# A hybrid decoder layer on one core: instructions kept in the order issued, the third weight sum in another tile, dependent work one piece later, one normalisation chain

## The chip, the cores and the metric

The kernel runs on one core of one Trainium2 chip. The metric is the device time of one execution in microseconds, given as the median of several runs. In the texts below PE is the matrix engine, DVE the vector engine, ACT the scalar engine, POOL the GpSimd engine and SP the engine from which most DMAs are issued. The engines run side by side, each through its own queue of instructions in order, and wait for one another by semaphores.

## The reference

The reference is one layer over 272 positions (16 learned ones and 256 given ones) of 4096 channels: a norm, one projection to 16384 columns, two branches (stick-breaking attention and a gated short convolution, sixteen heads of 128 each), each multiplied by a gate and normalised per head, and one projection back, added to the input and normalised.

```python
h = rmsnorm(x, norm_g)
p = h @ w_in                                   # 272 x 4096 by 4096 x 16384
q, k, v, g_attn, b_conv, c_conv, h_conv, z_conv = jnp.split(p, cuts, axis=-1)
o = stick_breaking_attention(heads(q), heads(k), heads(v))
o = group_rmsnorm(o * jax.nn.silu(g_attn), attn_norm_g, ATTN_HEADS)
y = b_conv * short_conv(c_conv * h_conv, conv_w)
y = group_rmsnorm(y * jax.nn.silu(z_conv), conv_norm_g, CONV_GROUPS)
hs = x + jnp.concatenate([o, y], axis=-1) @ w_out
return rmsnorm(hs, final_norm_g)[:, N_META:]
```

All in fp32. Attention takes, for each query, weights worked out from the scores by a logarithm, a reversed running sum and an exponential.

## The kernel before

**Pieces.** The weights come as a list of pieces, 128 x 1024 numbers each, and one loop (L916) goes through the list. Piece `i` is multiplied in round `i`; its load was issued eight pieces ahead (`LOADS`), its split five ahead (`SPLITS`). A split (`split`, L345) makes two fp32r tiles out of an fp32 piece: `wh`, a cast by ACT (L381), and `wl`, what the cast left out, a subtraction by DVE (L382). Each product is then three matmuls: `wh` with both parts of the activations, `wl` with the large one (L414, L416, L417 for rows, L406 to L408 for blocks). The raw tiles have five buffers, `wh` and `wl` six.

**Kinds of pieces.** The columns q, gate, b and z of a pair of heads (a *group*, eight in all) are computed with positions as rows. Two row blocks of the weight make a *pair*. A plain pair is two pieces A and B of four products each, twelve matmuls a piece. A "seven" pair uses a scheme with seven products in place of eight: A (2), B (1), T (2), U (2). T and U are not loaded but summed by DVE from A's and B's raw tiles, in three sums (L391, L394, L395): T into a tile `t` that has one buffer, U back into A's raw tile. The columns k, v, c and h of each head are computed with channels as rows: a *block* of 272 or 258 positions, in four *quarters* p of 8 row blocks, 24 matmuls each. Pieces x give the norm's statistics, pieces m load the mixed output of a group back, and eight pieces o make the last thin output columns.

**Zones.** A group from the second on begins with zone R: four plain pairs, between them the last four half blocks of the group before (its second head's c and h), sixteen pieces, called f+1 to f+16 after the last piece f of the group before. Then comes zone S, twelve *slots*, numbered 0 to 11, each the A, B, T and U of a seven pair and two quarters of a block, so that a block ends in every odd slot: k, v, c, h of the first head and k, v of the second. After the last group stand its last two blocks (zone Z), and then the second projection, with its own pairs.

**Work around the pieces.** At the end of a block `plain_block` reads its PSUM bank by DVE: `kT` (L545), `vt` (L551), `cc` (L567), and `cc` multiplied (L572) for the block h. After the last plain piece `open_rows` copies one finished bank into `cb` (ACT, L604); at the end of the group `evict` reads the others. The rest is done in tasks. `later(at, fn)` puts one down for round `at`, and `run_tasks`, the last call of each round, issues those that are due, each whole. `plan_group` (L777) sets the rounds. For group g: `silu` and the transposes `qT` at f+1; for each of its two heads `scores`, `weights`, `trans` and `po`, the second head's at f+10, f+13, f+15 and f+18; the normalisation of its attention part (`norm`, "h") at f+20. In zone S of the group after: `conv_t` (four transposes `ct`) in slot 2, `conv_out` (POOL) one round on, the normalisation of its convolution part ("c") and the mix of h (`mxh`) in slot 4, the mix of c (`mxc`) in slot 8. The last group has rounds of its own.

`trans` transposes the attention weights in blocks of 32 (DVE) and moves the blocks to their places in `at` by sixteen ACT copies (L538); `po` (L740 to L744) multiplies them with `vv`, the transposed v, which comes by sixteen copies of the same kind and four of `v3` (L560) after each v block. A `norm` is four squares (ACT, L653), a chain of eleven small DVE operations (L655, `rsqrt_raw`, L657) and four multiplications (ACT, L660). A `mix` is four transposes on PE (L666), whose result ACT multiplies by the norm's weights (L677) and sends to memory.

**PSUM banks.** In zone S seven banks hold the group's products, and the eighth, the *spare* bank, is taken in turn by each block and by the transposes `ct`, `mxh`, `mxc` and the second head's `po`. A new user waits until the one before has been read.

**What sets the order.** The instructions of an engine do not run in the order in which the code issues them: the framework's scheduler puts each engine's queue in an order of its own, by its estimate of when each instruction's operands are ready. A waiting instruction holds all behind it in that queue.

Of the kernel before, what the change touches and what calls it, by code (L numbers as in the profile page):

```python
# [110 lines left out]
def kernel(ctx, tc, xt, xin, xm, par, fg, w1, w2, out):  # L111
# [124 lines left out]
    def small(nm):  # L236
        return [wk.tile([P, 4], F32, tag=f"sm{i}", name=f"{nm}{i}") for i in range(3)]
# [9 lines left out]
    xr, kept = {}, {}  # L247
# [30 lines left out]
    def late_sums(j):  # L278
# [5 lines left out]
        token_sums(d, t, j)  # L284
        kept[j] = d

    def lend(j):

        nc.sync.dma_start(out=sumd[j], in_=kept.pop(j).bitcast(F32))

    def token_sums(dst, t, j):
# [7 lines left out]
        v.tensor_tensor(out=f[:, 3, :], in0=a12, in1=f[:, 1, :], op=ALU.add)  # L299
        nc.scalar.copy(out=dst[:, 0], in_=f)  # L300
# [44 lines left out]
    def split(i):  # L345
# [9 lines left out]
        if p[0] == "m":  # L355
# [4 lines left out]
            for q in range(2):  # L360
                j = 2 * p[1] + q
                if j in OUT_SJ:
# [4 lines left out]
                    token_sums(S2[j], t[:, 2 * q:2 * q + 2], f"o{j}")  # L367
# [8 lines left out]
        else:  # L376
            h = wp.tile([P, 1024], F32R, tag="wh", name=f"wh{i}", bufs=RING)
            lo = wp.tile([P, 1024], F32R, tag="wl", name=f"wl{i}", bufs=RING)
        for q in range(parts):
            c = slice(q * w // parts, (q + 1) * w // parts)  # L380
            nc.scalar.copy(out=h[:, c], in_=t[:, c])  # L381
            nc.vector.tensor_tensor(out=lo[:, c], in0=t[:, c], in1=h[:, c].bitcast(F32), op=ALU.subtract)  # L382
        splits[i] = (h, lo)
        if two and p[0] == "A":
            sums[p] = t
        elif two:
# [7 lines left out]
            nc.vector.tensor_tensor(out=a[:, c2], in0=a[:, c2], in1=s[:, c1], op=ALU.add)  # L394
            nc.vector.tensor_tensor(out=a[:, c1], in0=t[:, c1], in1=a[:, c2], op=ALU.add)  # L395
            sums[("T",) + p[1:]], sums[("U",) + p[1:]] = s, a

# [92 lines left out]
    tasks = []  # L490
# [4 lines left out]
    def run_tasks(i):  # L495
        ready = [t for t in tasks if t[0] <= i]
        for t in ready:
            tasks.remove(t)
        for t in sorted(ready, key=lambda t: t[0]):
            t[1](*t[2])  # L500
# [3 lines left out]
    def finish_stats():  # L504
        sst = wk.tile([P, 4], F32, tag="sm3", name="sst")
# [42 lines left out]
    def v_block(u, src, at_):  # L548
# [4 lines left out]
        def vtrans():  # L553
            y = wk.tile([P, 416], F32, tag="zs", name=f"yv{u}")
            V.transpose(out=y[:, :L + META], in_=vt[:, :L + META])
            vv = wk.tile([P, 2 * P], F32, tag=f"vv{u % 2}", name=f"vv{u}")
# [88 lines left out]
    def norm(g, q):  # L645

        y = gr[g][q][1]
        f = 0 if q == "h" else 4
        ss = wk.tile([P, 4], F32, tag="sm3", name=f"ss{q}{g}")
        j = wk.tile([P, P], F32, tag="junk", name=f"j{q}{g}")  # L650
        for t in range(2):
            for u in range(2):
                A.activation(out=j, in_=y[:, t, u], func=AF.Square, scale=(rt if q == "h" else rt2)[:, t:t + 1],  # L653
                             accum_out=ss[:, 2 * u + t:2 * u + t + 1])
        V.tensor_scalar(out=ss, in0=ss, scalar1=1.0 / P, scalar2=None, op0=ALU.mult)  # L655
        r = rsqrt_raw(ss, 4, EPS, *small(f"n{q}{g}_"))
        V.tensor_tensor(out=ss, in0=r, in1=fac[:, f:f + 4], op=ALU.mult)  # L657
        for t in range(2):
            for u in range(2):
                A.mul(out=y[:, t, u], in_=y[:, t, u], mul=ss[:, 2 * u + t:2 * u + t + 1])  # L660
# [23 lines left out]
    def q_t(g):  # L684
        q = gr[g]["h"][0]
        o = bank(f"qT{g}")
        for u in range(2):
            for t in range(2):
                c = (2 * u + t) * P
                T.transpose(out=o[:, c:c + P], in_=q[:, t, u], identity=ident)  # L690
        A.copy(out=q, in_=o.rearrange("p (u t x) -> p t u x", u=2, t=2))

    def scores(g, u):
# [4 lines left out]
        T.matmul(out=z[:, 144:ZW], lhsT=q[:, 1, u], rhs=kt, start=True, stop=True)  # L698
        zm = wk.tile([P, 448], F32, tag="zm", name=f"zm{g}_{u}")[:, :ZW]
# [18 lines left out]

# [10 lines left out]
    def trans(g, u):  # L729
        za = gr[g].pop(("za", u))  # L730
        y = wk.tile([P, 448], F32, tag="zl", name=f"ya{g}_{u}")
        V.transpose(out=y, in_=za)
        blocks(at[:, P:], y[:, :3 * P], 3)
# [16 lines left out]
    def conv_t(us):  # L750
        o = bank(f"ct{us[0]}")
        for n, u in enumerate(us):
            for t in range(2):
                T.transpose(out=o[:, n * SEQ + t * P:n * SEQ + (t + 1) * P], in_=cy[u][:, t * P:(t + 1) * P], identity=ident)
# [292 lines left out]
```

## Time and profile before

| | |
|---|---|
| median of 3 runs | 1840.49 us (1839.96 to 1843.44) |
| profiled execution, its own time | 1845.58 us |
| its span, first to last instruction | 1843.9 us |
| mean granted clock of PE | 0.994 |
| DMA | 393.64 MB, 213 GB/s on average |

The profile describes one execution, which took 5.1 us longer than the median of the runs. Its page gives the busy time of each engine as a share of the span. The groups list the instructions of one line, engine and operation, with the busy time and the mean duration of one, and then the idle time just before them and which engine's work ended it. A timeline row has the start in us, the duration, engine, line, operation and tiles (`out<-in`), and how many instructions it holds. A windows row has for each engine its busy time in that stretch (PE, weight loads, DVE, ACT, POOL), the granted clock of PE as a share of full speed, the DMA engines' share and GB/s.

### The profile page before, as it was taken

What the parts mean: (1) busy time and instruction counts of PE and PEld (TensorE: products, weight loads), DVE (VectorE), ACT (ScalarE), POOL (GpSimd) and SP (SyncE); (2) the same over time, 40 slices, a digit from 0 to 9 for tenths busy, and PEclk for the clock granted to TensorE, in tenths of its full rate; (3) what the DMA queues carried; (4) which work ended last, traced back from release to release, by engine and by line L of the source; (5) the groups of instructions that cost most, each with busy time, mean ns of one, the idle gap of its engine ahead of it and who ended that gap; (6) DMA issues with size and microseconds to landing.
All of it is one profiled execution on the core that took longest, in us unless ns stands there. A gap on an engine that the chain in (4) does not pass through costs nothing.

```text
span 1843.9 us, 29709 instructions
## 1 busy us (share of the span) xinstructions
PE 1793.4 (97%) x10998; PEld 1618.1 (88%) x10998; DVE 1493.0 (81%) x1946; ACT 1201.2 (65%) x2012; POOL 154.2 (8%) x192
## 2 busy tenths in 40 slices
PE   9999999999999999999999999999999998999997
PEld 7899888988898889888988898889888976888897
DVE  6765788778877887888788877887788878998986
ACT  6755875686568656865776577657765785554554
POOL 2150010101010101010101010101010231000000
PEclk9999999999999999999999999999999999999999
DMA  8867467746765677467746674667466774675655
GB/s 308 318 237 239 162 195 235 230 169 198 225 225 175 199 230 231 165 206 226 239 161 209 222 235 166 210 211 234 161 211 212 236 271 160 228 227 191 208 180 194
DMA packets 116065, 393.64 MB, mean 213 GB/s; under 512 B 13008, under 2 KB 18256, under 8 KB 115920
## 3 DMA queue, kind: packets, MB, share of 16 engines
q1 hardware_dynamic: 111888, 388.08, 64.2%
q10 hardware_dynamic: 4032, 3.67, 0.6%
q8 instruction: 86, 1.41, 0.3%
q14 instruction: 59, 0.48, 0.1%
HBM read 380.17 MB, written 11.53 MB: 212 GB/s over the span
## 4 chain that ended last, share of the span: by engine, by line
PE 74%; DVE 9%; issue 5%; ACT 5%; DMA 3%; POOL 2%; SPq 0%; ACTq 0%; DVEq 0%; POOLq 0%
PE P L414 14%; PE P L416 14%; PE P L417 14%; PE mm L406 10%; PE mm L407 10%; PE mm L408 10%; DVE wl L382 4%; ACT wh L381 3%; DMA raw<-w 2%; DVE t L391 1%; DVE raw L395 1%; DVE raw L394 1%; ACT at L538 1%; POOL cb L643 1%; PE mo L860 0%
## 5 line engine op out<-in xcount | busy, mean ns | idle before, releaser
L382 DVE TENSOR_TENSOR wl<-raw,wh 128x1024 fp32r<-128x1024 f32 (+3 forms) x756 | 846.0, 1150 | 228.3 <-ACT wh L381 219.0
L381 ACT CAST wh<-raw 128x1024 fp32r<-128x1024 f32 (+3 forms) x756 | 708.1, 974 | 385.8 <-DVE raw L395 213.2
L406 PE MATMUL mm<-xs,wh 128*128 128x258 f32 (+1 forms) x2048 | 584.9, 286 | 0.0
L408 PE MATMUL mm<-xs,wl 128*128 128x258 f32 (+1 forms) x2048 | 581.7, 284 | 0.6 <-DVE wl L382 0.6
L407 PE MATMUL mm<-xs,wh 128*128 128x258 f32 (+1 forms) x2048 | 581.9, 284 | 0.0
L406 PEld LDWEIGHTS mm<-xs,wh 128*128 128x128 f32 x2048 | 385.6, 188 | 5.8 <-issue 0.6
L407 PEld LDWEIGHTS mm<-xs,wh 128*128 128x128 f32 x2048 | 385.7, 188 | 4.4
L408 PEld LDWEIGHTS mm<-xs,wl 128*128 128x128 f32 x2048 | 385.6, 188 | 0.8 <-DVE wl L382 0.8
L414 PE MATMUL P<-wh,xs 128*128 128x512 f32 x604 | 237.6, 393 | 1.5 <-ACT wh L381 1.5
L417 PE MATMUL P<-wl,xs 128*128 128x512 f32 x604 | 235.7, 391 | 0.7 <-DVE wl L382 0.5
L416 PE MATMUL P<-wh,xs 128*128 128x512 f32 x604 | 235.7, 390 | 0.0
L391 DVE TENSOR_TENSOR t<-raw,raw 128x1024 f32<-128x1024 f32 (+1 forms) x108 | 130.2, 1206 | 32.5 <-DMA raw<-w 32.3
L381 ACT CAST wh<-t 128x1024 fp32r<-128x1024 f32 (+1 forms) x108 | 112.0, 1037 | 58.9 <-DVE t L391 21.7
L414 PE MATMUL P<-wh,mixl 128*128 128x512 f32 (+1 forms) x392 | 148.4, 379 | 0.0
L416 PE MATMUL P<-wh,mixh 128*128 128x512 f32 (+1 forms) x392 | 147.5, 377 | 0.0
L417 PE MATMUL P<-wl,mixh 128*128 128x512 f32 (+1 forms) x392 | 147.2, 377 | 0.0
L382 DVE TENSOR_TENSOR wl<-t,wh 128x1024 fp32r<-128x1024 f32 (+1 forms) x108 | 130.8, 1211 | 6.9 <-ACT wh L381 6.3
L417 PEld LDWEIGHTS P<-wl,xs 128*128 128x128 f32 x604 | 113.6, 188 | 25.6 <-DVE wl L382 1.5
L414 PEld LDWEIGHTS P<-wh,xs 128*128 128x128 f32 x604 | 113.8, 188 | 21.8 <-ACT wh L381 2.1
L416 PEld LDWEIGHTS P<-wh,xs 128*128 128x128 f32 x604 | 113.7, 188 | 20.0
L414 PEld LDWEIGHTS P<-wh,mixl 128*128 128x128 f32 x392 | 74.0, 189 | 11.9 <-ACT wh L381 0.4
L417 PEld LDWEIGHTS P<-wl,mixh 128*128 128x128 f32 x392 | 73.9, 188 | 12.1 <-DVE wl L382 0.3
(257 smaller groups left out, 2097.0 us busy)
## 6 DMA issues: line engine op xcount, KB each, us to landing
raw<-w SPq DMA_DIRECT2D x614, 512.0 KB, 4.3
lent<-sumd SPq DMA_DIRECT2D x49, 512.0 KB, 4.6
raw<-w SPq DMA_DIRECT2D x32, 384.0 KB, 3.5
raw<-xin SPq DMA_DIRECT2D x8, 512.0 KB, 5.3
xr<-xt SPq DMA_DIRECT2D x15, 272.0 KB, 5.0
sumd<-lent SPq DMA_DIRECT2D x7, 512.0 KB, 3.8
raw<-mixd SPq DMA_DIRECT2D x7, 512.0 KB, 4.4
res<-xin SPq DMA_DIRECT2D x12, 256.0 KB, 5.0
```

The source lines that it names most:

```text
L381: nc.scalar.copy(out=h[:, c], in_=t[:, c])
L382: nc.vector.tensor_tensor(out=lo[:, c], in0=t[:, c], in1=h[:, c].bitcast(F32), op=ALU.subtract)
L391: nc.vector.tensor_tensor(out=s[:, :2 * hw].rearrange("p (a b) -> p a b", a=2), in0=a[:, :2 * hw].rearrange("p (a b) -> p a b", a=2), in1= ...
L394: nc.vector.tensor_tensor(out=a[:, c2], in0=a[:, c2], in1=s[:, c1], op=ALU.add)
L395: nc.vector.tensor_tensor(out=a[:, c1], in0=t[:, c1], in1=a[:, c2], op=ALU.add)
L406: nc.tensor.matmul(out=o, lhsT=h, rhs=x[:, 0, s:], start=k == 0, stop=False)
L407: nc.tensor.matmul(out=o, lhsT=h, rhs=x[:, 1, s:], start=False, stop=False)
L408: nc.tensor.matmul(out=o, lhsT=lo, rhs=x[:, 0, s:], start=False, stop=k == KC - 1)
L414: nc.tensor.matmul(out=o, lhsT=a[1], rhs=h, start=key not in begun, stop=False)
L416: nc.tensor.matmul(out=o, lhsT=a[0], rhs=h, start=False, stop=False)
L417: nc.tensor.matmul(out=o, lhsT=a[0], rhs=lo, start=False, stop=last)
L538: A.copy(out=o, in_=x)
```

## The change

From the second round after group 0's last product up to the eighth piece from the end, the program is in a stretch (`tc.manual_schedule()`) in which each engine's instructions stand in the order in which the code issues them. With it the code issues things in another order:

- The split of piece i+5 follows the matmuls of piece i and stands ahead of `plain_block`, `evict` and the tasks of that round.
- In a seven pair the second sum goes into B's raw tile and the third too, so that U lies there and A's tile is free after the second sum. The order on DVE is t, second sum, `wl` of B, third sum.
- A task may be a generator: `yield k` ends its part of this round, and the rest is issued k pieces later. `vtrans`, `q_t`, `scores`, `weights`, `trans`, `po`, `conv_t` and `mix` put the second half of their work, which reads what the first half makes, one piece later.
- The two normalisations of a group become one chain of DVE operations on eight columns. The squares of h stand at f+20, those of c in slot 4 (f+19 in the last group), the chain one piece after slot 4 (f+21), the multiplications of h one piece later, of c two. The mix of h moves from slot 4 to slot 6 (f+23 in the last group), the mix of c stays in slot 8 (f+24 in the last group).
- The token sums that are written to memory (`late_sums`) are spread over several rounds, the DMA with them; those of the second projection (`kept_sums`) too. The squares of the output have four small tiles instead of two and are added up some pieces later.

```diff
-    def norm(g, q):
+    def squares(g, q):
...
                 A.activation(out=j, in_=y[:, t, u], func=AF.Square, scale=(rt if q == "h" else rt2)[:, t:t + 1],
-                             accum_out=ss[:, 2 * u + t:2 * u + t + 1])
+                             accum_out=ss[:, c:c + 1])
+
+    def norm(g):
+
+        ss = gr[g]["ss"]
         V.tensor_scalar(out=ss, in0=ss, scalar1=1.0 / P, scalar2=None, op0=ALU.mult)
-        r = rsqrt_raw(ss, 4, EPS, *small(f"n{q}{g}_"))
-        V.tensor_tensor(out=ss, in0=r, in1=fac[:, f:f + 4], op=ALU.mult)
-        for t in range(2):
-            for u in range(2):
-                A.mul(out=y[:, t, u], in_=y[:, t, u], mul=ss[:, 2 * u + t:2 * u + t + 1])
+        r = rsqrt_raw(ss, 8, EPS, *small(f"n{g}_"))
+        V.tensor_tensor(out=ss, in0=r, in1=fac, op=ALU.mult)
+        for f, q in ((0, "h"), (4, "c")):
+            yield 1
+            y = gr[g][q][1]
+            for t in range(2):
+                for u in range(2):
+                    c = f + 2 * u + t
+                    A.mul(out=y[:, t, u], in_=y[:, t, u], mul=ss[:, c:c + 1])
...
-            nc.vector.tensor_tensor(out=lo[:, c], in0=t[:, c], in1=h[:, c].bitcast(F32), op=ALU.subtract)
+            if not two or p[0] == "A":
+                low(c)
...
-            nc.vector.tensor_tensor(out=a[:, c2], in0=a[:, c2], in1=s[:, c1], op=ALU.add)
-            nc.vector.tensor_tensor(out=a[:, c1], in0=t[:, c1], in1=a[:, c2], op=ALU.add)
-            sums[("T",) + p[1:]], sums[("U",) + p[1:]] = s, a
+            nc.vector.tensor_tensor(out=t[:, c2], in0=a[:, c2], in1=s[:, c1], op=ALU.add)
+            low(c1)
+            nc.vector.tensor_tensor(out=t[:, c1], in0=t[:, c1], in1=t[:, c2], op=ALU.add)
+            sums[("T",) + p[1:]], sums[("U",) + p[1:]] = s, t
...
+            g = t[2] if t[1] is None else t[1](*t[2])
+            if g is not None:
+                k = next(g, None)
+                if k is not None:
+                    tasks.append((after(i, k), None, g))
...
         V.transpose(out=y, in_=za)
+        yield 1
         blocks(at[:, P:], y[:, :3 * P], 3)
...
             mix_t(g, q, u, o[:, u * SEQ:(u + 1) * SEQ])
+        yield 1
         mix_out(g, q, (0, 1), o)
...
-        later(after(f, 20), norm, g, "h")
-        later(after(f, 24) if end else slot(g + 1, 4), mix, g, "h")
         e = ends[2 * g + 1, 3]
         later(after(e, 4) if end else slot(g + 1, 2), conv_t, (2 * g, 2 * g + 1))
-        later(after(e, 5) if end else slot(g + 1, 2) + 1, conv_out, g)
-        later(after(e, 9) if end else slot(g + 1, 4), norm, g, "c")
-        later(after(e, 14) if end else slot(g + 1, 8), mix, g, "c")
+        later(after(e, 6) if end else after(slot(g + 1, 2), 2), conv_out, g)
+        later(after(f, 20), squares, g, "h")
+        later(after(f, 19) if end else slot(g + 1, 4), squares, g, "c")
+        later(after(f, 21) if end else after(slot(g + 1, 4), 1), norm, g)
+        later(after(f, 23) if end else slot(g + 1, 6), mix, g, "h")
+        later(after(f, 24) if end else slot(g + 1, 8), mix, g, "c")
...
+        if i == top[0] + 1:
+            fixed = ExitStack()
+            fixed.enter_context(tc.manual_schedule())
+        if i == n - 8:
+            fixed.close()
...
         if i < n1:
             mm_in(i)
+            while halved < until:
+                split(halved)
+                halved += 1
             if p[0] == "p" and p[2] == 3:
                 plain_block(*p[1], i)
...
-            while halved < until:
-                split(halved)
-                halved += 1
             if i == n1 - 1:
                 open_tail()
```

Three places of the queues show it. ACT's queue at the end of zone R of group 2 (`P_2` is the bank that the last plain piece finishes, `za_1` and `ya_1` belong to the second head's attention weights), before:

```order
L538 COPY at<-ya_1_4270 32x3x32 x5
L381 CAST wh_4266<-raw_4046 128x1024
L538 COPY at<-ya_1_4270 32x3x32 x11
L381 CAST wh_4311<-raw_4169 128x1024
L381 CAST wh_4322<-raw_4221 128x1024
L604 COPY cb_4309<-P_2_3875 128x512
L381 CAST wh_4329<-raw_4252 128x1024
```

and now:

```order
L764 ACTIVATE za_1_4233<-zs_1_4196 128x16
L399 CAST wh_4253<-raw_4064 128x1024
L399 CAST wh_4278<-raw_4156 128x1024
L629 COPY cb_4282<-P_2_3862 128x512
L562 COPY at<-ya_1_4257 32x3x32 x16
L399 CAST wh_4309<-raw_4201 128x1024
L399 CAST wh_4316<-raw_4239 128x1024
```

The sixteen copies to `at`, ahead of the copy of `cb` before, now stand right behind it.

DVE's queue at the end of a first head's block h, in slot 7 of the same group (`raw_5115` and `raw_5146` are the A and B of one pair, `t_5205` its T; `cc` reads the block's bank), before:

```order
L394 TENSOR_TENSOR raw_5115<-raw_5115,t_5205 128x512
L382 TENSOR_TENSOR wl_5218<-t_5205,wh_5217 128x1024
L395 TENSOR_TENSOR raw_5115<-raw_5146,raw_5115 128x512
L382 TENSOR_TENSOR wl_5248<-raw_5115,wh_5247 128x1024
L382 TENSOR_TENSOR wl_5279<-raw_5193,wh_5278 128x1024
L391 TENSOR_TENSOR t_5327<-raw_5221,raw_5251 128x1024
L572 TENSOR_TENSOR cc_5062<-mm_3_5117,cc_5062 128x258
```

and now:

```order
L409 TENSOR_TENSOR t_5176<-raw_5087,raw_5118 128x1024
L412 TENSOR_TENSOR raw_5118<-raw_5087,t_5176 128x512
L395 TENSOR_TENSOR wl_5174<-raw_5118,wh_5173 128x512
L414 TENSOR_TENSOR raw_5118<-raw_5118 128x512
L395 TENSOR_TENSOR wl_5190<-t_5176,wh_5189 128x1024
L395 TENSOR_TENSOR wl_5220<-raw_5118,wh_5219 128x1024
L395 TENSOR_TENSOR wl_5250<-raw_5165,wh_5249 128x1024
L597 TENSOR_TENSOR cc_5027<-mm_3_5089,cc_5027 128x258
```

The first sum of the next pair no longer stands ahead of the read, and U is summed ahead of T's split.

ACT's queue around slot 4 of group 1 (`cb_927` and `cb_931` hold group 0's convolution part, `vv` and `v` belong to group 1's first head), before:

```order
L381 CAST wh_2756<-raw_2701 128x512
L660 ACTIVATE cb_927<-cb_927,ssc_2867 128x128
L381 CAST wh_2772<-t_2760 128x1024
L660 ACTIVATE cb_927<-cb_927,ssc_2867 128x128
L381 CAST wh_2802<-raw_2670 128x1024
L381 CAST wh_2835<-raw_2748 128x1024
L381 CAST wh_2845<-raw_2764 128x1024
L381 CAST wh_2852<-raw_2776 128x1024
L538 COPY vv_2893<-yv_2891 32x2x32 x3
```

and now:

```order
L399 CAST wh_2836<-raw_2760 128x1024
L681 ACTIVATE jc_2840,ss_2418<-cb_931,rt_125 128x128 x4
L399 CAST wh_2855<-raw_2790 128x512
L562 COPY vv_2877<-yv_2845 32x2x32 x16
L585 COPY v_2894<-yv_2845 16x32 x4
L399 CAST wh_2907<-t_2858 128x1024
L696 ACTIVATE cq_932<-cq_932,ss_2418 128x128 x4
L399 CAST wh_2944<-raw_2790 128x1024
L696 ACTIVATE cb_931<-cb_931,ss_2418 128x128 x4
```

Squares, copies and both sets of multiplications, spread among casts before, now stand within five casts.

More of the change, by code (lines that the diff above doesn't have):

```diff
@@ L236, in small @@
     def small(nm):
-        return [wk.tile([P, 4], F32, tag=f"sm{i}", name=f"{nm}{i}") for i in range(3)]
+        return [wk.tile([P, 8], F32, tag=f"sm{i}", name=f"{nm}{i}") for i in range(3)]
     xctx = ExitStack()
@@ L378, in split, with low @@
             lo = wp.tile([P, 1024], F32R, tag="wl", name=f"wl{i}", bufs=RING)
+        splits[i] = (h, lo)
+        def low(c):
+            nc.vector.tensor_tensor(out=lo[:, c], in0=t[:, c], in1=h[:, c].bitcast(F32), op=ALU.subtract)
         for q in range(parts):
@@ L495, in run_tasks @@
     def run_tasks(i):
-        ready = [t for t in tasks if t[0] <= i]
-        for t in ready:
-            tasks.remove(t)
-        for t in sorted(ready, key=lambda t: t[0]):
-            t[1](*t[2])
+        while True:
+            ready = [t for t in tasks if t[0] <= i]
+            if not ready:
+                return
+            t = min(ready, key=lambda t: t[0])
+            tasks.remove(t)
+            g = t[2] if t[1] is None else t[1](*t[2])
[3 more added lines that the diff above has]
+                    tasks.append((after(i, k), None, g))
     V, A, G, T = nc.vector, nc.scalar, nc.gpsimd, nc.tensor
     def finish_stats():
-        sst = wk.tile([P, 4], F32, tag="sm3", name="sst")
+        sst = wk.tile([P, 8], F32, tag="sm3", name="sst")
         V.tensor_reduce(out=sst[:, 0:1], in_=sq9[:, 0:4], axis=AX.X, op=ALU.add)
@@ L805, in open_tail @@
         acc.extend(tp.tile([P, 1], F32, name=f"acc{t}") for t in range(2))
-        sqs.extend(tp.tile([P, 1], F32, name=f"sq{t}") for t in range(2))
+        sqs.extend(tp.tile([P, 1], F32, name=f"sq{t}") for t in range(4))
         fgs["pool"] = tp
@@ L873, in out_block, with add_up @@
         if 0 < nb < 8:
-            V.tensor_tensor(out=acc[t], in0=acc[t], in1=sqs[t], op=ALU.add)
+            later(after(now[0], 2 * (nb % 2) + t + 1), add_up, nb, t, q)
+    def add_up(nb, t, q):
+        V.tensor_tensor(out=acc[t], in0=acc[t], in1=q, op=ALU.add)
         if nb == 7:
@@ L922 @@
         until = min(i + SPLITS + ahead + 1, n)
-        while halved < until - (0 <= i < n1):
+        while i < 0 and halved < until:
             split(halved)
@@ L959 @@
         elif p[0] == "o":
+            while halved < until:
+                split(halved)
+                halved += 1
             if "all" not in hd:
```

60 lines of the change are left out of this document (40 added, 20 removed).

## The prediction

> **What bounds the kernel now.** First the page's busy times, for the engine that sets the end.
>
> ```profile
> span 1843.9 us, 29709 instructions
> ...
> PE 1793.4 (97%) x10998; PEld 1618.1 (88%) x10998; DVE 1493.0 (81%) x1946; ACT 1201.2 (65%) x2012; POOL 154.2 (8%) x192
> ```
>
> PE is busy for 1793.4 of 1843.9 us, so at most 50.5 us can be won by feeding it better; the matmuls stay the same. DVE and ACT count only where PE waits for them. Next the groups by line, for PE's idle time (last column) and what ended it:
>
> ```profile
> L414 PE MATMUL P<-wh,osum 128*128 128x512 f32 (+1 forms) x96 | 36.7, 382 | 2.4 <-DVE mixl L682 2.4
> ...
> L740 PE MATMUL po<-vv,at 128*128 128x128 f32 x32 | 7.0, 299 | 3.3 <-ACT cb L604 1.9 <-ACT at L538 1.4
> ...
> L666 PE MATMUL mxh<-ident,cq 128*128 128x128 f32 x32 | 5.6, 296 | 12.0 <-DVE vt L551 7.3 <-ACT cq L660 4.7
> L666 PE MATMUL mxc<-ident,cb 128*128 128x128 f32 x32 | 5.5, 297 | 14.4 <-DVE cc L572 14.4
> L754 PE MATMUL ct<-ident,cy 128*128 128x128 f32 x32 | 5.4, 286 | 3.7 <-DVE kT L545 2.0 <-DVE cy L580 1.8
> ```
>
> That is 35.8 of the 50.5 us. They are small jobs of the per-head work that stand in PE's queue between the large products. The waits on `cc`, `vt` and `kT` are for the bank: in zone S the transposes use the PSUM bank of the block that has just ended, so DVE must first read that block out. Parts of the windows view give a second cost, the granted clock (second last but two columns, 1.00 or 0.50):
>
> ```profile
> 490.00:493.40 3.40, 1.14 (x7) 1.06 (x8) 3.37 (x5) 2.08 (x5) 0.00 (x0) 1.00 0.80 213
> 493.40:496.80 3.40, 3.40 (x9) 2.67 (x8) 3.40 (x7) 1.41 (x2) 0.00 (x0) 0.50 0.84 205
> 1537.90:1541.30 3.40, 1.01 (x5) 0.48 (x3) 3.33 (x7) 1.67 (x4) 0.00 (x0) 1.00 0.00 0
> 1541.30:1544.70 3.40, 3.36 (x8) 2.71 (x9) 2.96 (x4) 2.30 (x3) 0.00 (x0) 0.50 0.49 154
> ```
>
> Where PE was busy for only about 1.1 of 3.4 us, the next 3.4 us run at half clock, which loses 1.7 us more. The trace has five such stretches inside the work: three after `mxc` waits in the groups and two near 1535 and 1541 us.
>
> **Units.** All sums are made against the profiled execution. PE's timeline in one slot:
>
> ```profile
> 1202.46 0.28 PE L406 MATMUL mm<-xs,wh 128*128 128x258 f32 x1
> ...
> 1208.18 0.40 PE L414 MATMUL P<-wh,xs 128*128 128x512 f32 x1
> ...
> 1212.96 0.28 PE L406 MATMUL mm<-xs,wh 128*128 128x258 f32 x1
> ```
>
> Between the first two rows stand the 48 matmuls of two block quarters, 5.72 us; between the last two the 21 products of A, B, T and U (6, 3, 6 and 6), 4.78 us, 0.227 each. A slot of zone S is thus 10.50 us of PE; A takes 1.36, A and B together 2.04.
>
> **What costs nothing by itself.** The third weight sum in the second raw tile, the wider small tiles and the split sums of squares change only DVE's and ACT's queues, which have PE's time to hide in. One chain of normalisation less takes eleven small DVE operations out of each group. But DVE's place in its queue when a block ends is what `mxc` waits for:
>
> ```profile
> 1212.87 1.23 DVE L391 TENSOR_TENSOR t<-raw,raw 128x1024 f32<-128x1024 f32 x1 [2.55 <-DMA raw<-w]
> ...
> 1220.50 2.36 DVE L382 TENSOR_TENSOR wl<-raw,wh 128x1024 fp32r<-128x1024 f32 x2 [1.19 <-ACT wh L381]
> 1222.82 1.23 DVE L391 TENSOR_TENSOR t<-raw,raw 128x1024 f32<-128x1024 f32 x1
> 1223.96 0.42 DVE L572 TENSOR_TENSOR cc<-mm,cc 128x258 f32<-128x258 f32 x1
> ```
>
> and on PE, at the end of the block:
>
> ```profile
> 1218.68 0.40 PE L414 MATMUL P<-wh,xs 128*128 128x512 f32 x1
> ```
>
> The block ended where A's first product starts (1218.68); DVE read it only at 1223.96, 5.3 us later, while PE wanted the bank 2.04 us later. Of the 5.3 us the change takes away 1.14 (`t` now stands behind the read), 1.19 (the third sum is made before T's split, so ACT has U's cast ready) and the 2.55 us wait for the raw tile (A's tile is free after the second sum). About 0.4 us is left, below 2.04. So **`mxc` falls from 14.4 to 0, and the seven `ct` from 2.0 to 0**, with DVE's splits as the cover.
>
> **The new wait: `po` behind `cb`.** The second head's `at` copies now follow the copy of `cb` on ACT, which waits until PE ends the last plain piece. Before, they were done ahead of it:
>
> ```profile
> 399.32 0.57 ACT L604 COPY cb<-P 128x512 f32<-128x512 f32 x1
> ...
> 1506.32 4.46 ACT L538 COPY at<-ya 32x96 f32<-32x96 f32 x16
> ```
>
> After that piece: 0.1 to be told, `cb` to the next start 0.47 (0.57 less the overlap of 0.1 that follows each ACT row), sixteen copies 4.46: 5.0 us. PE has only A and B of slot 0, 2.04 us, before `po`, and its queue is in order, so T waits too. It idles 3.0 us in each of seven groups: 21.0 against 1.9 now, **+19.1**. Nothing can cover it.
>
> **The clock.** An idle time of 3.0 us puts 1.9 us or more into one of the fixed 3.4 us stretches in about five places of six; six of the seven then cost 1.7 us. The three stretches after `mxc` go: 6 x 1.7 - 3 x 1.7 = **+5.1**.
>
> The Trainium skill ("TensorE: Matmul & The Clock Gate", Part 1) gives a free-running window of 3413 ns and a return to half rate after at least one idle window. The stretches agree with the window; the rows above contradict the full idle window, since a third of it was busy. By the page none of the seven would be slowed; that is rival C.
>
> **`mxh`, moved from slot 4 to slot 6.** It now follows slot 5. But slot 4 gets a burst on ACT: the squares of c, the sixteen `vv` and four `v3` copies of the first head, and both multiplications, all in the order issued.
>
> ```profile
> 1462.01 4.04 ACT L538 COPY vv<-yv 32x64 f32<-32x64 f32 x16
> 1466.06 0.90 ACT L560 COPY v<-yv 16x32 f32<-16x32 f32 x4
> ...
> 1497.59 2.00 ACT L381 CAST wh<-raw 128x1024 fp32r<-128x1024 f32 x2
> ...
> 1505.39 0.40 ACT L653 ACTIVATE jc<-cb,rt 128x128 f32<-128x128 f32 x1
> ...
> 1512.71 1.27 ACT L660 ACTIVATE cb<-cb,ssc 128x128 f32<-128x128 f32 x4
> ```
>
> A cast steps at 0.95 (2.00 less 1.05; half of that for B), four squares at 1.9 (two lie between 1505.39 and 1506.32). From the cast of slot 5's A to that of its first quarter: 4 x 0.95 + 0.5 + 1.9 + 4.04 + 0.90 + 2 x 1.2 = 13.5 us. It can begin when PE leaves A (1.36 us into slot 4, plus 0.1), so it ends at 15.0; DVE's split of that quarter takes 1.15 more: 16.1. PE wants it at 10.50 + 4.78 + 0.24 = 15.5. **PE waits 0.6, with the hand-over 0.8 us: +5.6** over seven groups, a wait that the trace before does not have; the bounds are 0 and 2 us.
>
> From there DVE has nine splits and sums before the read of block c:
>
> ```profile
> 439.24 0.68 DVE L394 TENSOR_TENSOR raw<-raw,t 128x512 f32<-128x512 f32 x1
> 439.84 1.22 DVE L382 TENSOR_TENSOR wl<-t,wh 128x1024 fp32r<-128x1024 f32 x1
> 440.98 0.68 DVE L395 TENSOR_TENSOR raw<-raw,raw 128x512 f32<-128x512 f32 x1
> ```
>
> Steps of 0.60 and 1.14: five splits and `t` at 1.14, three of half width at 0.60, and the read 0.42 make 9.1; DVE is through at 25.2. PE wants the bank at 15.3 + 0.8 + 5.72 + 2.04 = 23.8. **`mxh` waits 1.4, with the hand-over 1.5 us**, 10.5 in seven groups against 7.3: **+3.2**. So the burst gives back what the move should win.
>
> **The last group's work**, near 1490 to 1545 us, now has its norm chain in one piece and mixes that no longer stand among late reads. Its waits are in the groups above: `ct` 1.8, `po` 1.4, `mxh` 4.7, `osum` 2.4, with two slowed stretches 13.7 us. I leave 3 (`po` still comes soon behind its copies): **-10.7**. It lies between -13.7 and 0.
>
> **Sum.** 19.1 + 5.1 + 5.6 + 3.2 - 14.4 - 2.0 - 10.7 = **+5.9 us**. The profiled execution took 1845.58 (span 1843.9 and 1.7 around it), so 1851.5 there; the median of the runs, 1840.49, is 5.1 lower, and I put the change on it: 1846.4, say **1847 us**.
>
> **Rivals.** The row for D is one of the windows view; the fourth sum in it is ACT's busy time.
>
> ```profile
> 1490.00:1500.00 10.00, 9.07 (x44) 7.55 (x45) 8.09 (x13) 9.88 (x18) 6.27 (x11) 1.00 0.86 278
> ```
>
> A, faster: the `at` copies are not late. Place: ACT at the end of zone R. To be in time they must begin 2.4 us before PE ends the last plain piece (4.46 less 2.04). Against it: the new order has `cb` ahead of them, and `cb` reads that piece's last product. The 19.1 and the six half-clock stretches (10.2) fall away: 1817.
>
> B, faster: the burst of slot 4 is absorbed. It decides at about 12.7 us from cast to cast. For it: the casts run five pieces ahead, and the trace before hides the `vv` copies in the same zone. Against it: the squares and the multiplications now come beside them. Then 5.6 and the 10.5 at `mxh` go: 1830.
>
> C: no half clock after the seven waits, 10.2 less: 1836. The stretch with 1.14 us of busy time speaks against it.
>
> D, slower: strict order leaves the last group's waits (10.7 back) and half of those at `mxc` (7.2 back): 1864. Place: ACT from 1490 us on, 9.88 of 10 us busy before, and now nothing overtakes an instruction that waits. It decides where ACT falls back by more than the five pieces that its casts run ahead.
>
> E: the third sum's new place alone changes nothing, as PE does not wait there; that lies inside the forecast.
>
> **Chances.** Forecast 0.42 (1838 to 1857), A 0.12, B 0.22, C 0.06, D 0.18. A measurement here can tell about 0.2%, 3.7 us, from no change. Faster by more: A, most of B, half of C, 0.34. Within: a low end of the forecast and parts of B and C, 0.17. Slower: 0.49. The range takes in half of A and most of D, 1822 to 1864; the forecast's own range is narrower.
>
> **What would show it.** Right: PE idle before `po` near 3 us, ended by ACT's `at` copies, in seven places; half clock behind most of them; `mxc` without idle time; a short wait for `wl` in slot 5 and `mxh` waiting on block c's read. Wrong: `po` waiting less than 1 us (A), no wait in slot 5 (B), no clock row of 0.5 there (C), or new waits for `wh` or `wl` elsewhere (D). A PE busy time that is not near 1793 us, clock apart, would upset the whole account.

## The result and the profile after

The changed kernel takes 1905.66 us, the median of four runs (1903.0 to 1906.97), against 1840.36 us for the kernel before (four runs, 1839.96 to 1843.44): 1.0349 times as long, with a 95% interval of 1.0331 to 1.0367. The forecast was 1847, with a range up to 1864. The change makes the kernel slower, by about ten times what was forecast. Further down, one execution of e1 (4589.2 us) and one of e6 (1957.63 us), far slower than the others of the same kernel, are left out of medians and ratios.

The page of the kernel after has the same number of matmuls in a longer span. PE's busy time is 25 us longer; most of that is the half clock worked out below:

```profile
span 1901.0 us, 29647 instructions
...
PE 1818.4 (96%) x10998; PEld 1633.5 (86%) x10998; DVE 1504.2 (79%) x1858; ACT 1204.9 (63%) x2012; POOL 146.7 (8%) x192
```

The groups by line on PE, with its idle time in the last column, answer to the groups of before:

```profile
L426 PE MATMUL mm<-xs,wl 128*128 128x258 f32 (+1 forms) x2048 | 582.6, 284 | 4.8 <-DVE wl L395 4.8
L432 PE MATMUL P<-wh,xs 128*128 128x512 f32 x604 | 239.1, 396 | 3.8 <-DVE cc L597 2.3 <-ACT wh L399 1.5
L779 PE MATMUL po<-vv,at 128*128 128x128 f32 x32 | 8.6, 357 | 39.3 <-ACT at L562 39.3
L702 PE MATMUL mxh<-ident,cq 128*128 128x128 f32 x32 | 5.0, 279 | 11.5 <-DVE cc L592 11.5
L702 PE MATMUL mxc<-ident,cb 128*128 128x128 f32 x32 | 4.8, 272 | 0.0
L793 PE MATMUL ct<-ident,cy 128*128 128x128 f32 x32 | 4.8, 271 | 0.0
```

`mxc` and `ct` wait no more, `mxh` waits about as long as before though elsewhere, 4.8 us for `wl` in slot 5 are new, and `po` went from 3.3 to 39.3 us. The starts of the same matmul in the two traces say where the time was lost:

| place | before, us | after, us | difference |
|---|---|---|---|
| last product ahead of the second head's `po`, first of seven times | 217.43 | 216.96 | -0.47 |
| first matmul of the last plain product, fifth time | 947.13 | 972.24 | +25.11 |
| last product ahead of `po`, fifth time | 949.62 | 975.31 | +25.69 |
| first matmul of `po`, fifth time | 950.24 | 979.95 | +29.71 |
| the 120th matmul behind that | 968.85 | 1001.31 | +32.46 |
| last product ahead of `po`, seventh time | 1316.89 | 1354.54 | +37.65 |
| first transpose `ct` of the last group | 1488.80 | 1530.36 | +41.56 |
| a product behind the last group's work | 1610.42 | 1665.24 | +54.81 |
| last matmul | 1832.80 | 1889.77 | +56.97 |

A group costs 38.1 / 6 = 6.35 us more; the last group's work 13 us from its first `ct` on; the last pieces 2.2. The four rows of the fifth time span the end of one zone R: 7.35 us are lost there, and some of it is won back in the zone S behind. Where a loss is given "by the starts" below, it comes from such rows, taken for every group and every run in the same way, against the kernel before.

The timeline at the end of zone R of that group, first PE, then ACT, then two rows of DVE:

```profile
975.31 0.39 PE L435 MATMUL P<-wl,xs 128*128 128x512 f32 x1
979.95 0.80 PE L779 MATMUL po<-vv,at 128*128 128x128 f32 x2 [4.25 <-ACT at L562]
```

```profile
971.81 0.42 ACT L761 ACTIVATE za<-zs 128x256 f32<-128x256 f32 x1 [1.87 <-DVE zs L755]
...
972.55 1.98 ACT L399 CAST wh<-raw 128x1024 fp32r<-128x1024 f32 x2
974.44 0.57 ACT L629 COPY cb<-P 128x512 f32<-128x512 f32 x1
975.43 4.47 ACT L562 COPY at<-ya 32x96 f32<-32x96 f32 x16 [0.42 <-DVE ya L770]
```

```profile
973.61 1.23 DVE L395 TENSOR_TENSOR wl<-raw,wh 128x1024 fp32r<-128x1024 f32 x1
974.75 0.64 DVE L770 STREAM_TRANSPOSE ya<-za 128x448 f32<-128x448 f32 x1
```

The last plain product ended at 973.08. The copy of `cb` did not start then but 1.36 us later, because ACT still had two casts to do, and these stood behind exponentials that had waited for DVE. The copies to `at` then waited another 0.42 us, not for `cb` but for the transpose `ya`, which stood behind a split on DVE. In the kernel before, the same exponentials began 9.2 us ahead of the copy of `cb` (here 2.6 us), and the copies to `at` were done when it came; in the second group, at 399.32:

```profile
390.14 0.42 ACT L723 ACTIVATE za<-zs 128x256 f32<-128x256 f32 x1
...
391.81 1.40 ACT L538 COPY at<-ya 32x96 f32<-32x96 f32 x5 [0.45 <-DVE ya L732]
...
394.31 3.08 ACT L538 COPY at<-ya 32x96 f32<-32x96 f32 x11
```

Then the clock, in four stretches of 3.41 us laid so that each has one clock throughout (PE, weight loads, DVE, ACT, POOL, granted clock):

```profile
975.28:978.69 3.41, 0.42 (x2) 0.00 (x0) 3.12 (x8) 3.13 (x12) 0.00 (x0) 1.00 0.49 154
978.69:982.10 3.41, 2.15 (x9) 1.93 (x9) 1.10 (x1) 3.34 (x8) 0.00 (x0) 0.50 0.84 293
982.10:985.52 3.42, 3.42 (x9) 2.62 (x10) 3.39 (x5) 0.59 (x2) 0.00 (x0) 0.50 0.55 173
985.52:988.93 3.41, 3.41 (x23) 2.88 (x22) 2.46 (x4) 3.08 (x10) 0.00 (x0) 1.00 0.45 154
```

The wait of 4.25 us lies in two stretches, and the clock is half from 978.69 to 985.52. By the table that costs 2.75 us more (+29.71 becomes +32.46). Half clock follows all seven of these waits, for two stretches six times and for three the last time; by the starts it costs 21.6 us in all.

In the last group `po` waits 7.40 us. ACT's rows (some between them are left out) show what came ahead of its copies:

```profile
1549.93 0.62 ACT L296 CAST osum<-sfo 128x512 fp32r<-128x512 f32 x1 [3.78 <-POOL sfo L308]
1550.57 1.28 ACT L761 ACT_TABLE_LOAD   x1
...
1556.43 4.47 ACT L562 COPY at<-ya 32x96 f32<-32x96 f32 x16
```

ACT stood 3.78 us for POOL's token sums with the second head's exponentials behind it.

### The profile page after: what moved, and what is told of

Same layout as the page of the kernel before. It is cut to its first block, busy times and chain, and to the rows that moved or that the text cites. A ratio compares the mean times of both kernels' runs of the same rounds, so it can differ in the third digit from the quotient of the medians.

```text
span 1901.0 us, 29647 instructions
## 1 busy us (share of the span) xinstructions
PE 1818.4 (96%) x10998; PEld 1633.5 (86%) x10998; DVE 1504.2 (79%) x1858; ACT 1204.9 (63%) x2012; POOL 146.7 (8%) x192
## 5 line engine op out<-in xcount | busy, mean ns | idle before, releaser
L395 DVE TENSOR_TENSOR wl<-t,wh 128x1024 fp32r<-128x1024 f32 (+1 forms) x108 | 131.7, 1220 | 12.2 <-ACT wh L399 12.2
L435 PEld LDWEIGHTS P<-wl,mixh 128*128 128x128 f32 x392 | 74.5, 190 | 16.3 <-DVE wl L395 4.4
L432 PEld LDWEIGHTS P<-wh,mixl 128*128 128x128 f32 x392 | 74.7, 191 | 14.4 <-DVE os L881 2.4
```

Of the source, the lines that this page charges most:

```text
L432: nc.tensor.matmul(out=o, lhsT=a[1], rhs=h, start=key not in begun, stop=False)
L435: nc.tensor.matmul(out=o, lhsT=a[0], rhs=lo, start=False, stop=last)
```

## The experiments

Each time is a median, each ratio (with its interval) is to the kernel before.

### The end of zone R

**e1**: the copy of `cb` behind the tasks of its round, so that the copies to `at` come first.

```diff
-            if i in plain_end.values():
-                open_rows(p[1])
...
         run_tasks(i)
+        if i in plain_end.values() and i > top[0]:
+            open_rows(p[1])
```

> The changed kernel with the copy of cb at the end of zone R issued after the tasks of that round, so that the sixteen at copies stand ahead of it on ACT. Theory 1 (the prediction's: the at copies are late because they stand behind the cb copy): po's wait falls from 4.24 us to at most 1 us in seven places and the half clock behind it goes, about 7 x (3.2 + 2.5) = 40 us less, 1866 us. Theory 2 (the second head's chain of weights itself ends too late: the transpose ya ended at 975.39, 0.04 us before the copies began): the copies gain 0.4 us at most, and since po takes the bank that the cb copy frees, po now waits for both, 4.0 to 5.0 us: 1903 to 1912 us.

Measured: 1912.53 us, 1.0397 (1.0362 to 1.0433). `po` waits 4.84 us each, now for `cb`. The copies stand ahead of it and still come late, when `ya` is there:

```profile
981.02 4.48 ACT L562 COPY at<-ya 32x96 f32<-32x96 f32 x16 [0.89 <-DVE ya L770]
```

The prediction's reason, that the copies are late because they stand behind `cb`, is false.

**e2**: the second head's chain one piece earlier.

```diff
+            d = 0 if end else 1
-            later(after(f, z), scores, g, u)
+            later(after(f, z - d), scores, g, u)
...
-            later(after(f, z + 5), trans, g, u)
+            later(after(f, z + 5 - d), trans, g, u)
```

> The changed kernel with scores, weights and trans of both heads one piece earlier, po where it was (not in the last group). Theory 2: the at copies end a piece (2.7 to 2.9 us) earlier, po's wait falls from 4.24 us to between 0.3 us (cb copy last) and 1.5 us, and most of the half clock goes with it: 7 x (2.7 + 2.5) = 36 us less or more, 1856 to 1870 us. Rival: the whole ACT queue is late at this place, not this chain; the copies then only change places with casts, PE waits for wh or wl instead, and the time stays above 1890 us.

Measured: 1912.38 us, 1.0381 (1.0349 to 1.0413). The rival holds, in another shape. The copies stand ahead of `cb` now, yet ran only at 977.00, and `po` waits 4.2 us for `cb` behind them:

```profile
977.00 4.48 ACT L562 COPY at<-ya 32x96 f32<-32x96 f32 x16 [0.91 <-DVE ya L770]
981.50 1.04 ACT L399 CAST wh<-raw 128x1024 fp32r<-128x1024 f32 x1
982.45 0.58 ACT L629 COPY cb<-P 128x512 f32<-128x512 f32 x1
```

**e9**: `po` behind T and U of slot 0 (with its read in the same round and the squares of h one piece later; of the edit the main line is shown).

```diff
-            later(after(f, z + 8), po, g, u)
+            later(after(f, z + (8 if end or not u else 10)), po, g, u)
```

> The changed kernel with the second head's po two pieces later, after T and U of slot 0 instead of ahead of them, and the squares of h one piece later (the last group as it is). Theory: the wait is the distance between the end of the at copies and PE's arrival, so 2.72 us more of products take it from 4.24 to about 1.5 us, with 0.8 us at most for wl of the quarter behind it, and the half clock goes: 7 x (1.9 to 2.7 + 2 to 2.5) = 27 to 36 us less, 1870 to 1879 us. Rival (as with the earlier chain, the late ACT queue passes the wait on to the next casts): PE waits for wh or wl in slot 0 for as long, above 1890 us.

Measured: 1927.62 us, 1.0463 (1.0439 to 1.0487). `po` waits 1.52 us, as expected; but the next block needs its bank, and DVE reads `po` behind all that was issued for that round:

```profile
992.26 2.36 DVE L395 TENSOR_TENSOR wl<-raw,wh 128x1024 fp32r<-128x1024 f32 x2 [2.46 <-ACT wh L399]
994.54 1.22 DVE L409 TENSOR_TENSOR t<-raw,raw 128x1024 f32<-128x1024 f32 x1
...
998.86 0.42 DVE L787 TENSOR_TENSOR cq<-po,cq 128x256 f32<-128x256 f32 x1
```

That is a new wait of 6.55 us in each group, which neither theory had.

**e12**: the splits of a round back behind the reads and the copy of `cb`, ahead of the tasks (the three lines of the loop, moved).

> The changed kernel with the splits of a round back behind plain_block, open_rows and evict, as the code stood before, still ahead of the tasks, fixed order throughout. Theory 7 (a block's read and the cb copy stand behind a split that waits for ACT): the reads come 1 to 2.5 us earlier, so mxh's wait falls from 1.64 us to at most 0.5 us and the 0.33 us for cc at slot 0 goes, but po still waits for the at copies: 8 to 16 us less, 1890 to 1898 us. Rival (an instruction that waits for PE at the head of ACT's and DVE's queues holds the casts behind it): new waits for wh or wl, above 1906 us.

Measured: 1912.02 us, 1.0374 (1.0357 to 1.0391). `mxh` falls from 11.5 to 3.5 us, as the theory has it, but the wait for `cc` at slot 0 stays (2.4 us) and `po` rises from 39.3 to 48.0, so that the time is on the rival's side.

**e15**: the scheduler's order in zone R alone.

```diff
-        if i == top[0] + 1:
+    starts = [slot(g, 1) for g in range(1, GROUPS)]
+    stops = [fin[g] + 1 for g in range(1, GROUPS - 1)] + [n - 8]
...
+        if i in starts:
...
-        if i == n - 8:
+        if i in stops:
```

> The changed kernel with the scheduler's order in the zones R alone (from the end of each group to slot 1 of the next), the fixed order in the zones S and from the last group on, mixes as changed. Theory 6 (the fixed order in zone R costs what po waits there and the half clock behind it, about 7 us a group): po's waits in the groups fall from 4.24 to at most 1.8 us, the half clock goes, and the time falls by 30 to 45 us, 1861 to 1876 us. Rival (the scheduler cannot make up for the later halves in zone R either): 1885 us or more.

Measured: 1884.17 us, 1.0227 (1.0204 to 1.0251): 21 us less than the changed kernel, short of the theory and close to the rival. `po` waits 1.7 to 2.0 us in the groups, 12.8 us in all, and half of the half clock stays. By the starts, the zones R cost 22 us against the kernel before, where they cost 54 in the changed kernel; the last pieces cost 6.6 us, not 2.2. What stays in zone R is in the code's order, from which the scheduler works (e17).

### The last group

**e3**: the token sums of the second projection by DVE.

```diff
-        v = nc.gpsimd
+        v = nc.vector if str(j)[0] == "o" else nc.gpsimd
```

> The changed kernel with the token sums of the second projection made by DVE instead of POOL (four small operations each). Theory 3 (in the last group ACT, in order, waits for POOL's sums, 3.78 us just ahead of the second head's exponentials, and passes that on to the at copies): the 7.4 us wait of po near 1553 us falls to 2 to 4 us and the span by 4 to 8 us, 1898 to 1902 us. Rival (any wait in that stretch only makes room for the next one; DVE gets six times 1.2 us more): within 3 us of 1905.7 us.

Measured: 1905.04 us, 1.0347 (1.0322 to 1.0372). `po`'s 7.40 us become 2.39, but its first wait grows from 2.29 to 3.13 and those of the products for `wl` from 4.9 to 7.0 us. Taking away one wait in line made room for the next, as the rival has it.

**e4**: the fixed order closed at the last group's end.

```diff
-        if i == n - 8:
+        if i == fin[GROUPS - 1] + 1:
             fixed.close()
```

> The changed kernel with the stretch of fixed order closed at the end of the last group's products, so that the scheduler orders the rest. Theory 4 (the last group's loss comes from the order as issued, since nothing overtakes an instruction that waits): the 13 us lost between 1495 and 1640 us go, and the 2 us at the last pieces, 1888 to 1894 us. Rival (the loss comes from the moved rounds, the squares, the one chain and the mixes side by side): at least 8 us of the 13 stay, 1899 us or more.

Measured: 1886.6 us, 1.0248 (1.0223 to 1.0272), 19 us less. The last group's loss is the order as issued; the moved rounds do no harm there: by the starts, the last group now costs 2.2 us less than in the kernel before.

### The order as a whole

**e5**: no fixed order, the code as changed (the line with `manual_schedule` taken out).

> The changed kernel with the fixed order taken away, nothing else: the scheduler orders every engine's queue from the code as changed. Theory 4 (nearly all of the loss is the order as issued): po's wait falls below 0.5 us in each group, the half clock behind it goes, and the time comes to 1832 to 1845 us. Rival (the other parts, one normalisation chain, moved mixes and later halves, cost by themselves): 1850 us or more, with waits before mxh and mxc.

Measured: 1859.55 us, 1.0099 (1.0071 to 1.0128). 46 of the 65 us are the fixed order; 18 us stay, with waits of 13.6 us at `po` (for `cb`) and 17.9 at `mxh` (for block c), the latter in place of those at `mxc`, which are 2.4 us. DVE's first sum waits 75.1 us for loads here, as in e6 below.

**e8**: the kernel before, in the fixed order.

> The kernel before with the fixed order alone, over the same stretch, its tasks whole and its splits where they were. Theory (the second halves one piece later are what makes the fixed order bearable, since without them ACT and DVE wait in line for each result): over 1930 us. Rival (the halves cost more than they save, since they put the at copies behind the cb copy): 1906 us or less.

Measured: 1983.13 us, 1.0766 (1.0736 to 1.0797). `po` waits 50.7 us, the products 37 us for `wh`. So the fixed order needs the code's order changed with it. That it is the later halves which make it bearable is likely but not shown: e8 lacks the other parts of the change too.

### The sums

**e6**: the kernel before with only the sums changed: the second and the third in B's tile, the split of B between them (that line is left out here).

```diff
-            nc.vector.tensor_tensor(out=a[:, c2], in0=a[:, c2], in1=s[:, c1], op=ALU.add)
-            nc.vector.tensor_tensor(out=a[:, c1], in0=t[:, c1], in1=a[:, c2], op=ALU.add)
+            nc.vector.tensor_tensor(out=t[:, c2], in0=a[:, c2], in1=s[:, c1], op=ALU.add)
...
+            nc.vector.tensor_tensor(out=t[:, c1], in0=t[:, c1], in1=t[:, c2], op=ALU.add)
```

> The kernel before with only the sums changed: second and third sum in B's raw tile, the split of B between them. The prediction's step (changes nothing by itself, since PE does not wait there): within 3.7 us of 1840 us, mxc waiting 14.4 us in all as before, give or take 4. Rival (A's tile free earlier and the read of cc earlier in DVE's queue): mxc's wait falls by half or more and the time to 1825 to 1835 us.

Measured: 1872.55 us, 1.0164 (1.014 to 1.0188). The prediction's step was wrong, and the rival had the sign wrong: the part alone costs some 30 us. The same kernel once more, with its profile:

> The same kernel as e6, once more for a profile that is not disturbed. It took 1872 us, 31 us more than before, where the prediction's step expected no change. Theory 5 (the new order of the sums, second sum and the split of B between t and the third sum, pushes U's or the next pieces' splits back in DVE's queue so that PE waits for the read of a block): waits before mxc, mxh and ct of 25 us or more in all, with half clock behind them. Rival (U in the tile that was loaded later keeps that tile longer, so that a load starts late and t waits for it): waits of PE for wh or wl, and DVE idle before t by a DMA for more than the 32 us of before.

Measured: 1865.18 us (one run). `mxc` waits 16.7 us, `mxh` 16.3 and 2.0, `ct` 2.2, `po` 6.9. So PE waits where theory 5 has it, for the reads of blocks, and hardly for `wh` or `wl` (3.2 us); but DVE shows the rival's sign. The group of the first sum, before and then in this kernel, has its idle time for the load of the raw tile, 32.3 against 95.7 us:

```profile
L391 DVE TENSOR_TENSOR t<-raw,raw 128x1024 f32<-128x1024 f32 (+1 forms) x108 | 130.2, 1206 | 32.5 <-DMA raw<-w 32.3
```

```profile
L392 DVE TENSOR_TENSOR t<-raw,raw 128x1024 f32<-128x1024 f32 (+1 forms) x108 | 130.3, 1206 | 100.1 <-DMA raw<-w 95.7 <-issue 3.2 <-DVE ssh L657 0.7
```

In the scheduler's queue the reads of the blocks stand behind that `t`, as `vt` does here:

```profile
820.23 1.23 DVE L392 TENSOR_TENSOR t<-raw,raw 128x1024 f32<-128x1024 f32 x1 [2.34 <-DMA raw<-w]
...
824.25 0.43 DVE L553 TENSOR_TENSOR vt<-mm,rstd 128x272 f32<-128x272 f32 x1
```

The new tile and the new order of the sums were not tried apart in the scheduler's order.

**e16**: the changed kernel with the sums back in A's tile (the reverse of the lines above).

> The changed kernel, fixed order throughout, with the second and third sum back in A's raw tile, in the same order of instructions. The prediction's step (the tile of the sums changes nothing by itself in the fixed order): within 4 us of 1905.7 us. Rival (the raw tile that is free earlier lets loads and t come earlier, and the reads behind t with them): t waits for the DMA as before and mxh, mxc or cc wait longer, 1910 us or more.

Measured: 1904.93 us, 1.0338 (1.0318 to 1.0359), no difference from the changed kernel. In the fixed order, where the read stands ahead of the next `t`, the tile does nothing: `t` waits 2.0 us for loads with the sums in A's tile and 2.3 with them in B's.

### Zone S

**e7**: the mix of h in slot 10 (`slot(g + 1, 10)` for `slot(g + 1, 6)`).

> The changed kernel with the mix of h moved on from slot 6 to slot 10 (the last group as it is). The prediction's step (mxh waits in slot 6 because DVE, late by the burst of ACT in slot 4, reads block c late): in slot 10 no burst stands ahead, mxh's wait falls from 11.5 us to at most 2 us, the 0.69 us wait for wl in slot 5 stays, and the time falls by 9 to 13 us, 1893 to 1897 us. Rival (DVE in order reads every block this late, whichever slot): mxh waits 7 us or more in all, 1901 us or more.

Measured: 1891.5 us, 1.027 (1.0246 to 1.0293), 14 us less: `mxh` waits 0.0.

**e10**: the fixed order in the zones S only, with e7's slot (as e15, but closed at the end of every group).

> The changed kernel with the fixed order only from slot 1 of each group to the end of its zone S, the scheduler elsewhere, and the mix of h in slot 10. Theory (the fixed order wins in zone S, where mxc and ct wait no more, and loses in zone R and in the last group): po's waits fall to below 0.5 us as in the kernel before, the last group costs about what it did before, 4.8 us for wl in slot 5 stay: 1840 less 14.4, 7.3, 2.0 and 5.1, plus 5.6 = 1817 us, 1812 to 1825 us. Rival (the scheduler's freedom in zone R needs DVE and ACT to be ahead there, and they come out of zone S late): po waits 1 to 2 us as in e5, or new waits at the borders: 1835 us or more.

Measured: 1837.48 us, 0.997 (0.9956 to 0.9985). The theory holds for zone S, where nothing waits but the 5.3 us for `wl`; the rival holds for zone R and for the time: `po` waits 12.2 us for `cb`, 1.75 each.

**e11**: e10 with the normalisation in slot 6.

> As e10, with the squares of c and the chain of normalisation in slot 6 and the multiplications behind it, instead of slot 4. The prediction's step (the burst of ACT in slot 4 makes PE wait 0.69 us for wl in slot 5): seven waits of 0.69 us go, 5 to 6 us less than e10. Rival (the burst only moves, with the multiplications ahead of mxc in slot 8): mxc or slot 7 waits as long, within 2 us of e10.

Measured: 1841.35 us, 1.0003 (0.999 to 1.0016). The wait in slot 5 goes, so it was this burst; but `mxc` waits 10.8 us, and the time is 3.9 us above e10's: the burst moved.

**e13**: e10 with e12's place of the splits.

> As e10 (fixed order in zone S only, mix of h in slot 10), with the splits behind the reads. Theory 7 in zone R: the cb copy comes ahead of one cast, po's wait falls from 1.75 to 0.7 us or less, 7 us less than e10, 1829 to 1832 us. Rival (the scheduler does not go by the order of the code here, or the fixed part loses as much): within 3 us of 1837.5 us or above it.

Measured: 1847.77 us, 1.0028 (1.0017 to 1.0039). `po` waits 16.5 us, more than in e10.

**e14**: e13 with the copies of `vv` and `v3` in slot 5.

> As e13, with the transpose of the first head's v and its twenty copies six pieces later, in slot 5 instead of slot 4 (from the second group on). The prediction's step (the burst of ACT in slot 4, of which these copies are 4.95 us, makes PE wait 0.69 us for wl in slot 5): the seven waits go, 4 to 6 us less than e13. Rival (the copies do the same harm where they come now, as the moved chain of normalisation did in e11): within 2 us of e13, with waits at mxc or in slots 6 and 7.

Measured: 1853.72 us, 1.0058 (1.0044 to 1.0072). The wait in slot 5 goes again (5.4 to 0.7 us), but the row products now wait 6.6 us for `wh` (2.2 in e13) and 4.4 for `wl` (0.2 in e13).

### A version that beats both

**e17**: e10 with whole tasks wherever the scheduler sets the order.

```diff
                 k = next(g, None)
+                while k is not None and i >= top[0] + 1 and not on[0]:
+                    k = next(g, None)
```

> As e10, with the tasks issued whole, not half a piece later, wherever the scheduler sets the order (zones R and the last group). Theory 8 (what is left of po's wait there, 1.75 us before the cb copy, comes from the later halves, which the scheduler takes as the code's order): the at copies come one cast earlier, po waits 0.2 to 0.7 us as in the kernel before, 7 to 10 us less than e10, 1827 to 1831 us. Rival (PE arrives there earlier than before because it no longer waits in zone S, and ACT's chain of weights is as long as ever): within 3 us of e10's 1837.5 us.

Measured: 1823.83 us, 0.9898 (0.988 to 0.9916), faster than the kernel before by 1.0%. Zone S has lost all waits but the one for `wl`, and `po` waits 0.2 us in most groups; the 4.4 us at `mxh` are in the last group:

```profile
L426 PE MATMUL mm<-xs,wl 128*128 128x258 f32 (+1 forms) x2048 | 582.5, 284 | 5.3 <-DVE wl L395 5.3
L781 PE MATMUL po<-vv,at 128*128 128x128 f32 x32 | 7.0, 299 | 3.9 <-ACT cb L631 2.5 <-ACT at L564 1.4
L704 PE MATMUL mxh<-ident,cq 128*128 128x128 f32 x32 | 5.5, 292 | 4.6 <-issue 4.4 <-ACT cq L698 0.2
```

So the 1.75 us that `po` waited in e10 came from the later halves: a task cut in two does harm where the scheduler sets the order. By the starts the zones R cost 0.6 us here against 15.1 in e10, half clock included, which is more than theory 8 forecast.

## Why the prediction was wrong

**`po` behind `cb`, +19.1: the place was right, the reason and the size were not.** The prediction took the end of the last plain piece as the moment from which ACT is free. ACT was late by then. The chain of the second head's weights (scores, logarithm, sums, exponentials, transpose) goes back and forth between ACT and DVE, each in line behind casts and splits, and the copies start when it ends. The seven waits are 29.6 us, not 21.0 (27.8 more than before by the starts, not 19.1); 0.33 us for block h's read, 2.3 in all, come on top. e1 shows that `cb` is not what held the copies; e15 and e17 that the fixed order in zone R, and then the halves, are.

**The clock, +5.1: mis-sized.** It took one slowed stretch of 1.7 us for six of the seven waits, on a limit of 1.9 us of idle time that no row shows (3.0 us would put that much into one stretch in about three places of four, not five of six). The waits were longer than a stretch, and half clock followed all of them for two stretches or three: 2.75 us in the group shown, 21.6 in seven, where 10.2 were forecast. Why the second stretch is slow too stays open. The Trainium skill ("TensorE: Matmul & The Clock Gate", Part 1) has half rate follow at least one idle window. The stretch 975.28 to 978.69 held 0.42 us of products and was not idle throughout, and the next ran at 0.50; the measurement decides, and rival C is out.

**The last group, -10.7: the step that failed outright.** It was argued that the mixes no longer stand among late reads, with 3 us left. The 1.8 us at `ct` did go. In place of the others came `po`'s 9.7 us, 4.4 for `wl` and half clock in six stretches (four from 1555.54 us on, one each from 1589.67 and 1603.33): +13, some 24 us off. The prediction looked at which waits go, and not at what stands in line ahead of each instruction of the new queue: POOL's sums ahead of the exponentials. Rival D had the place and the direction, but priced it as a gain that stays away, not as a loss. e4 settles the cause (the order); e3 shows that taking away its longest wait alone gains nothing.

**Zone S: right, with its prices close.** `mxc` 14.4 to 0 and `ct` 2.0 to 0, as forecast; 4.8 us for `wl` in slot 5 (5.6 forecast), 11.5 at `mxh` (10.5 forecast). The burst as their cause was tested: without the copies (e14) or the normalisation (e11) in slot 4 the wait there goes; in slot 10 (e7) `mxh` waits for nothing. Of the reasons for `mxc`, the share put down to the free raw tile falls: with the old tile (e16) it is 0 as well. The order of DVE's queue did it; its two parts, `t` behind the read and the third sum ahead of T's split, were not tried apart.

**"The third sum costs nothing by itself":** true in the fixed order (e16), false in the scheduler's (e6), which the prediction's case E had ruled out.

**Not foreseen:** 2.2 us at the last pieces, where PE waits 1.9 us for DVE (`res`, L876). Whether that comes from the border of the fixed order was not tried alone; in e4 and e17 the wait is not there.

In sum, the starts split the 57.0 us between the last matmuls so: the ends of the seven zones R +53.6 (`po` 27.8, the clock 21.6, the read of block h 4.2), where +29 were forecast; the stretches between them, with the zones S, -11.0, where -13 were; the last group +13.3, where -11 were; the last pieces +2.2; and -1.1 ahead of all. So the end of zone R and the last group were each off by 24 us.

## What to carry to other kernels

In this kernel a fixed order paid where the chain between engines is short and known (block, read, next bank) and lost where work goes to and fro between engines; fix it by stage, and read in each stage what stands ahead of every instruction on which the critical engine waits. When a wait is taken away in an in-order queue, ask at once which instruction is then late: seven of the experiments moved a wait and did not remove it. Price a long wait together with the half clock behind it: here seven waits, 27.8 us longer in all than before, brought 21.6 us of it.

## What the runs showed of the hardware

Half clock came in whole stretches of 3.41 us. It followed stretches in which PE was busy for 0.42 us (975.28 above), for 1.08 and even for 1.71 us, and did not follow another with 1.59 us, so the busy time alone does not tell. After one `po` a stretch in which PE was busy throughout, at half clock, was followed by another at half clock:

```profile
408.66:412.08 3.42, 1.08 (x8) 0.97 (x8) 0.93 (x4) 3.30 (x11) 0.00 (x0) 1.00 0.52 171
412.08:415.49 3.41, 3.41 (x9) 2.64 (x9) 3.41 (x3) 1.41 (x2) 0.00 (x0) 0.50 0.69 237
415.49:418.90 3.41, 3.41 (x11) 2.56 (x10) 3.34 (x6) 2.28 (x7) 0.00 (x0) 0.50 0.53 191
418.90:422.32 3.42, 3.42 (x29) 3.42 (x29) 1.40 (x2) 2.36 (x6) 0.00 (x0) 1.00 0.07 22
...
1599.91:1603.33 3.42, 1.71 (x7) 1.03 (x7) 3.33 (x5) 2.41 (x3) 0.00 (x0) 1.00 0.60 199
1603.33:1606.74 3.41, 3.41 (x10) 2.64 (x9) 3.41 (x4) 2.70 (x4) 0.00 (x0) 0.50 0.95 241
...
1634.05:1637.46 3.41, 1.59 (x7) 1.33 (x8) 3.34 (x6) 1.04 (x1) 0.00 (x0) 1.00 0.94 382
1637.46:1640.88 3.42, 3.42 (x17) 2.83 (x16) 3.38 (x5) 0.11 (x1) 0.00 (x0) 1.00 0.43 147
```

Waits of 1.64 us at `mxh` were followed by no half clock; those of 4.24 us at `po` by 6.83 us of it, and once by 10.24.
